# A hybrid convolution and attention block: attention output gated inside its units, one of two masks replaced by value differences, other starting points for attention and layer norm

## The chip, the cores and the metric

The kernel runs on one core of one Trainium2 chip. The metric is device time in microseconds (us) for one launch; three runs were taken before the change, and one further run was profiled. Engines are named as in the profile: PE is TensorE (PEld is its weight load), DVE is VectorE, ACT is ScalarE, POOL is GpSimd, and SP is SyncE, whose queue issues the DMAs.

## The reference

One decoder block over 2048 tokens of width 1024, in float32:

```python
h = rmsnorm(x, norm_g)
glu_in, conv_gate, q, k, v, attn_gate, merge_logits = split(h @ w_in)      # 7680 columns
c = silu(layernorm(causal_depthwise_conv31(a * sigmoid(b)) + b_dw))        # a, b = halves of glu_in
y_conv = (c * silu(conv_gate)) @ w_conv_out
a = attention(rope(q), rope(k), v)      # 16 heads of 64, 4 KV heads, window 128, a sink logit per head
y_attn = (a * silu(attn_gate)) @ w_attn_out
g_conv, g_attn = split(sigmoid(merge_logits))
x = x + (g_conv * y_conv + g_attn * y_attn) @ w_out
return rmsnorm(x, final_norm_g)
```

With a window of 128 and blocks of 128 queries, query q of a block sees key j of its own block where j <= q, and key j of the block before where j > q: 128 keys in all, one for each j.

## The kernel before

**Tiling.** The tokens are worked in two sweeps of 1024 (`sweep(s)`), and each sweep in two halves of 512. Activations lie transposed, channels on the partitions. Every float32 product is made of three float32r passes: a high and a low part are kept of both operands (`put_split`, `split_lo`; the low part is "full minus high"), and hi*hi, hi*lo and lo*hi are added in PSUM. A projection (`project`) takes 48 matmuls of 128x512: 8 channel blocks, 3 passes, 2 halves. Its result leaves PSUM through an `ev` function on ACT or DVE.

**Stages of a sweep.** First k, v and q with their rotary embedding (`rope_items`, `v_item`; item 12 of the list of items is the first gate), mixed with the GLU pairs (`gb` and `ga`, eight of them, at the places in `GLU_AFTER`). Then four kinds of gates (`ag`, `cg`, `ma`, `mc`, eight projections each), each written to DRAM by `gate_item` and read back by `load_gate`. Then `ya` (attention output times w_attn_out), `yc` (convolution branch times w_conv_out) and `o` (times w_out) with the final norm.

**What runs beside the projections.** `Line` keeps a clock in estimated us of PE work and decides where in PE's order other work is written. PE's order is exactly the written one; the order on the other engines and on SP is made by the framework's scheduler. In the background list `bg`, one operation is written every `line.every` us: the depthwise convolution (`conv_ops`, 31 DVE operations of 128x1024 for each of 8 channel blocks), later layer norm (`ln_center`, `ln_recip`, `ln_apply`) and the preparation of operands (`a_ops`, `u_ops`). Attention is 32 units a sweep (4 KV heads times 8 blocks), one every `ATT_EVERY`, each in three steps with `LAT` between them:

1. `sc`: 8 matmuls of scores; DVE lays the two blocks' scores into one 128x512 tile `ss` (by `copy_predicated`), takes the maximum; ACT takes exponentials and normalises.
2. `tpp`: 4 transposes; ACT and DVE split the result into `pt`; POOL makes `pc` (own block's part) from `pt` by one `affine_select`, and masks `pt` itself (block before) by a second one.
3. `ov`: 4 matmuls with `v_of(g, b)` and `v_of(g, b - 1)`, then ACT and DVE add the parts to `oT`, which is written to DRAM (`spill["att"]`).

**The operand of `ya`.** `a_op(e, h)` loads a half block of attention output (`latt`) and of its gate (`lag`) into two of the five `t2k` buffers, multiplies them on DVE, copies the high part on ACT and subtracts on DVE, into `aT[h][e]`. The 16 of them are written after the last unit, 14 through `bg` and 2 once layer norm has ended. `ya_item(0, True)` empties all lists (`line.finish()`) before its first matmul. The slots `AT[0]` to `AT[15]` hold the units' tiles and later `aT`.

Of the kernel before, what the change touches and what calls it, by code (L numbers as in the profile page):

```python
# [51 lines left out]
def hybrid_block(ctx: ExitStack, tc: tile.TileContext, x, par_d, w_in, w_conv, sinks, w_attn, w_out,  # L52
# [93 lines left out]
    def lnb(c):  # L146
# [10 lines left out]
    v_halo = const.tile([P, NKV, 2, HD], F32R, name="v_halo")


    class Line:  # L160
# [38 lines left out]
        def after(self, us, chain):  # L199
            self.late.append((self.t + us, chain, lambda: True))  # L200
# [162 lines left out]
    def sweep(s):  # L363
# [6 lines left out]
        glu_slot = [C[7], C[6], C[5], C[4], AT[14], AT[15], C[7], AT[14]]  # L370
# [71 lines left out]
        def rope_items(name, e, store):  # L442
# [7 lines left out]
            def ev_b(half, ps):  # L450
                a = first[half]
                b = slot(AT[6], [P, 2, TH], F32, f"rb{s}_{name}_{half}")
# [25 lines left out]
        vt = {}  # L478

        def v_item(i):  # L480
            def chain(half, vs):
                yield 0.0, 7.0
                tp = tp_ps.tile([P, 4, P], F32, tag="tp", name=f"tpv{s}_{i}_{half}")
                for j in range(4):
                    pe.transpose(out=tp[:, j, :], in_=vs[:, j * P:(j + 1) * P], identity=ident)
                for j in range(2):
# [3 lines left out]
                    src = tp[:, 2 * j:2 * j + 2, :].rearrange("p b (g d) -> p b g d", d=HD)  # L490
                    hi, lo = (vt[bp][:, :, 2 * i:2 * i + 2, a * HD:(a + 1) * HD] for a in range(2))
                    act.copy(hi, src)
                    split_lo(lo, src, hi, dve)
# [33 lines left out]

        def attention(n):
            g, b = divmod(n, NB)
            u = f"{s}_{g}_{b}"  # L530
# [14 lines left out]
            oT = ss[:, 512:768].rearrange("p (a q) -> p a q", q=P)  # L545
# [23 lines left out]
            for h in range(GQ):  # L569
                pe.transpose(out=tpp[:, h, :], in_=sb[:, h, :], identity=ident)  # L570
            pt = slot(next_of("pt", AT[7:9]), [P, 2, GQ, P], F32R, f"pt{u}")
# [4 lines left out]
            else:  # L576
# [3 lines left out]
                pool.affine_select(out=pt, in_=f(pt), pattern=[[0, 2], [0, GQ], [-1, P]],  # L580
                                   compare_op=ALU.is_gt, fill=0.0, base=0, channel_multiplier=1)
                seq = [(v_of(g, b), pc), (v_of(g, b - 1), pt)]
# [8 lines left out]
            for r, own, other in ((0, slice(0, HD), slice(HD, P)), (1, slice(HD, P), slice(0, HD))):  # L591
                act.copy(oT[own], ovp[other, :, r, :])
                dve.tensor_tensor(out=oT[own], in0=ovp[own, :, r, :], in1=oT[own], op=ALU.add)
# [58 lines left out]
        def ln_chain():  # L652
# [3 lines left out]
            ln["mu"] = slot(AT[15], [P, T], F32, f"mu{s}")  # L656
# [7 lines left out]
        def ln_chain2():  # L664
# [3 lines left out]
            ln["r"] = slot(AT[14], [P, T], F32, f"rstd{s}")  # L668
# [12 lines left out]
        line.every = CONV_EVERY  # L681
# [236 lines left out]
```

## Time and profile before

| | us |
|---|---|
| three runs | 2933.14, 2132.34, 2133.77 |
| median | 2133.77 |
| the profiled execution | 2133.61 |
| its span, first to last instruction | 2131.9 |

| engine | busy us | share of the span | instructions |
|---|---|---|---|
| PE | 2075.1 | 97% | 9256 |
| DVE | 1404.9 | 66% | 1804 |
| ACT | 1008.8 | 47% | 2195 |
| POOL | 576.8 | 27% | 396 |

The mean granted clock of PE was 0.978 of full speed. PE's matmuls are pipelined, so that its busy share also counts stretches in which it advances slowly; the number of matmuls in a stretch, the granted clock and the list of waits say more. What lies outside the span (1.7 us) belongs to the launch.

### The profile page before, as it was taken

How to read it: one execution, taken by the hardware profiler on the slowest of the kernel's cores; microseconds unless marked ns; L12 is line 12 of the kernel's file. 1: busy time of each engine (PE TensorE's matmuls, PEld its weight loads, DVE VectorE, ACT ScalarE, POOL GpSimd, SP SyncE). 2: the span in 40 equal slices, each digit the busy share in tenths (PEclk: the TensorE clock that was granted, in tenths of full speed). 3: DMA queues.
4: the chain of work that ended last, by engine and by line, in shares of the span. 5: the costliest groups of instructions: out<-in, count | busy, mean ns of one | idle time of the engine just before them, and what ended most of it. 6: DMA issues, size and time to landing. Idle time of an engine off the chain costs nothing.

```text
span 2131.9 us, 27345 instructions
## 1 busy us (share of the span) xinstructions
PE 2075.1 (97%) x9256; PEld 1680.3 (79%) x9256; DVE 1404.9 (66%) x1804; ACT 1008.8 (47%) x2195; POOL 576.8 (27%) x396
## 2 busy tenths in 40 slices
PE   7999999999999989999999999999999999899998
PEld 6877778888788865888888888888888888478887
DVE  4999997797693747123568899796696664351224
ACT  6211256666658863122442123767666779331222
POOL 2445534444443431242001121222222211000200
PEclk9999999999999996999999999999999999799999
DMA  7343554545446458545344356454555554774431
GB/s 249 129 138 120 159 168 136 173 134 158 150 136 185 149 177 266 163 143 212 109 149 139 119 172 189 149 161 138 157 153 150 167 149 144 241 249 135 142 125 79
DMA packets 231515, 339.11 MB, mean 159 GB/s; under 512 B 26576, under 2 KB 92240, under 8 KB 231376
## 3 DMA queue, kind: packets, MB, share of 16 engines
q1 hardware_dynamic: 231376, 337.37, 49.8%
q8 instruction: 73, 1.20, 0.2%
q14 instruction: 66, 0.54, 0.1%
HBM read 226.12 MB, written 111.15 MB: 158 GB/s over the span
## 4 chain that ended last, share of the span: by engine, by line
PE 76%; DVE 6%; DMA 3%; ACT 2%; issue 1%; POOL 0%; SPq 0%; DVEq 0%; ACTq 0%; POOLq 0%
PE o L839 8%; PE mm_yc L273 8%; PE mm_ma L273 8%; PE mm_ag L273 8%; PE mm_ya L273 8%; PE mm_ga L273 6%; PE mm_cg L273 6%; PE mm_gb L273 6%; PE mm_mc L273 5%; DVE cv L384 3%; DMA latt<-d_att 2%; PE sc L542 2%; PE ov L589 2%; PE mm_q_a L273 2%; PE mm_q_b L273 2%; PE tpp L570 1%
## 5 line engine op out<-in xcount | busy, mean ns | idle before, releaser
L384 DVE SCALAR_TENSOR_TENSOR cv<-glu,par,cv 128x1024 f32<-128x1024 f32 x480 | 694.9, 1448 | 7.6
L578 POOL TENSOR_SCALAR_AFFINE_SELECT pc<-pt 128x1024 fp32r<-128x1024 f32 x60 | 91.3, 1521 | 436.9 <-DVE pt L234 394.6
L273 PE MATMUL mm_ya<-aT,whi_ya 128*128 128x512 f32 x512 | 184.8, 437 | 21.8 <-ACT aT L287 19.6
L839 PE MATMUL o<-wo,mT 128*128 128x512 f32 x768 | 180.8, 394 | 0.0
L273 PE MATMUL mm_ga<-hT,whi_ga 128*128 128x512 f32 x512 | 163.4, 401 | 5.4 <-DVE rb_q__1_1318 L454 3.4
L839 PEld LDWEIGHTS o<-wo,mT 128*128 128x128 f32 x768 | 143.3, 188 | 31.5
L273 PE MATMUL mm_gb<-hT,whi_gb 128*128 128x512 f32 x512 | 161.8, 397 | 0.0
L273 PE MATMUL mm_ag<-hT,whi_ag 128*128 128x512 f32 x512 | 160.7, 395 | 0.0
L273 PE MATMUL mm_cg<-hT,whi_cg 128*128 128x512 f32 x512 | 160.7, 395 | 0.0
L273 PE MATMUL mm_ma<-hT,whi_ma 128*128 128x512 f32 x512 | 160.6, 395 | 0.0
L273 PE MATMUL mm_mc<-hT,whi_mc 128*128 128x512 f32 x512 | 160.2, 394 | 0.0
L273 PE MATMUL mm_yc<-uT,whi_yc 128*128 128x512 f32 x512 | 159.4, 392 | 0.0
L273 PEld LDWEIGHTS mm_ya<-aT,whi_ya 128*128 128x128 f32 x512 | 103.1, 201 | 71.2 <-ACT aT L287 38.3
L560 ACT ACTIVATE ss<-ss,st 128x128 f32<-128x128 f32 x256 | 99.9, 391 | 102.2 <-DVE st L555 101.4
L273 PEld LDWEIGHTS mm_ga<-hT,whi_ga 128*128 128x128 f32 x512 | 96.0, 191 | 27.2 <-issue 6.2
L273 PEld LDWEIGHTS mm_yc<-uT,whi_yc 128*128 128x128 f32 x512 | 96.2, 188 | 21.9
L273 PEld LDWEIGHTS mm_gb<-hT,whi_gb 128*128 128x128 f32 x512 | 95.8, 190 | 20.6
L273 PEld LDWEIGHTS mm_mc<-hT,whi_mc 128*128 128x128 f32 x512 | 95.1, 188 | 20.5
L776 POOL TENSOR_TENSOR lmc<-lmc,mp 128x512 f32<-128x512 f32 x32 | 42.0, 1311 | 253.8 <-DVE lmc L775 249.7
L273 PEld LDWEIGHTS mm_ag<-hT,whi_ag 128*128 128x128 f32 x512 | 94.4, 188 | 19.7
L273 PEld LDWEIGHTS mm_ma<-hT,whi_ma 128*128 128x128 f32 x512 | 94.4, 188 | 19.5
L273 PEld LDWEIGHTS mm_cg<-hT,whi_cg 128*128 128x128 f32 x512 | 94.1, 188 | 19.3
(357 smaller groups left out, 4420.1 us busy)
## 6 DMA issues: line engine op xcount, KB each, us to landing
qk<-d_q SPq DMA_DIRECT2D x256, 64.0 KB, 2.6
qk<-d_k SPq DMA_DIRECT2D x240, 64.0 KB, 2.4
raw_gb<-in_w_in_dram SPq DMA_DIRECT2D x34, 256.0 KB, 3.1
raw_ga<-in_w_in_dram SPq DMA_DIRECT2D x34, 256.0 KB, 3.9
raw_ag<-in_w_in_dram SPq DMA_DIRECT2D x32, 256.0 KB, 3.4
d_ag<-ag SPq DMA_DIRECT2D x32, 256.0 KB, 2.1
d_att<-ss SPq DMA_DIRECT2D x64, 128.0 KB, 2.1
raw_cg<-in_w_in_dram SPq DMA_DIRECT2D x32, 256.0 KB, 3.1
```

The lines of the kernel that those rows point to most:

```text
L273: pe.matmul(out=ps, lhsT=a, rhs=b, start=(k == 0 and i == 0), stop=(k == KC - 1 and i == 2))
L384: dve.scalar_tensor_tensor(out=cv[c], in0=glu[c][:, j:j + T], scalar=tap(c, j), in1=cv[c], op0=ALU.mult, op1=ALU.add)
L542: pe.matmul(out=o, lhsT=q[:, h, :], rhs=r, start=(j == 0), stop=(j == 1))
L560: act.activation(out=sb[:, h, :], in_=sb[:, h, :], func=AF.Exp, scale=SCALE, bias=ngm[:, h:h + 1], accum_out=den[:, h:h + 1])
L570: pe.transpose(out=tpp[:, h, :], in_=sb[:, h, :], identity=ident)
L578: pool.affine_select(out=pc, in_=f(pt), pattern=[[0, 2], [0, GQ], [1, P]], compare_op=ALU.is_ge, fill=0.0, base=0, channel_multiplier=-1)
L589: pe.matmul(out=ov, lhsT=vv, rhs=pp[:, i % 2], start=(i == 0), stop=(i == nm - 1))
L776: pool.tensor_tensor(out=g, in0=g, in1=mp[e][:, half * TH:(half + 1) * TH], op=ALU.add)
L839: pe.matmul(out=ps, lhsT=a[:, c0:c0 + P], rhs=r, start=(k == 0 and i == 0), stop=(k == KC - 1 and i == 2))
```

## The change

- **Gating in the unit.** Step 2 of a unit loads its piece of the attention gate (`ga`, 128x256) into a free part of `ss`. After `ov`, DVE multiplies `oT` by it, ACT copies the high part and DVE subtracts the low part, and both go to a new DRAM array `d_a`. `a_op` is now one DMA of 512 KB straight into `aT[h][e]`. Steps 2 and 3 of a unit are held until the gate's projection is stored.
- **Value differences.** With P the probabilities by j, the output is the sum over all j of P times v(block before), plus the sum over j <= q of P times (v(own block) - v(block before)). So `pt` stays unmasked, one `affine_select` (for `pc`) is left, and `v_item` makes the differences `vd` beside `vt`, in three new slots `X` and in `AT[15]`.
- **Order.** `GLU_AFTER`, the spacing constants and `LAT` change; the first unit falls into the first gate projection as before, but three GLU pairs stand ahead of it now, not four. `ROPE_EVERY` 3.2 holds until the units are planned, `CONV_EVERY` from there.
- **Layer norm** keeps its mean and scale in `X[0]` and `X[1]`; `ln_apply` is put at the end of the background list; the `u` operands are begun from a list of their own; `ya_item(0)` empties the lists only where an operand was not yet written.
- The GLU tiles take turns in three slots, the rotary part `rb` in two, and the GpSimd's DMA scratch is made smaller to make room.

```diff
-LN_LAT = (14.0, 30.0)
-LN_EVERY = 2.4
-GLU_AFTER = (0, 4, 8, 12, 16, 20, 24, 28)
+LN_LAT = (14.0, 24.0)
+LN_EVERY = 1.6
+GLU_AFTER = (0, 6, 12, 16, 19, 22, 25, 28)
+ROPE_EVERY = 3.2
 CONV_EVERY = 2.4
-ATT_EVERY = 14.5
-LAT = (22.0, 14.0)
+ATT_EVERY = 13.8
+LAT = (22.0, 16.0)
...
-        glu_slot = [C[7], C[6], C[5], C[4], AT[14], AT[15], C[7], AT[14]]
+        glu_slot = [C[7], C[6], AT[14], C[7], C[6], AT[14], C[7], AT[14]]
...
+                vf, d = (t2k(f"{n}{s}_{i}_{half}").rearrange("p (b c) -> p b c", c=P) for n in ("vf", "vd"))
+                act.copy(vf, tp)
+                dve.tensor_tensor(out=d[:, 1:4], in0=tp[:, 1:4], in1=vf[:, 0:3], op=ALU.subtract)
+                dve.tensor_tensor(out=d[:, 0], in0=tp[:, 0], in1=v_last[:, i], op=ALU.subtract)
+                act.copy(v_last[:, i], vf[:, 3])
...
+                    for full, to in ((tp, vt), (d, vd)):
+                        part = full[:, 2 * j:2 * j + 2, :].rearrange("p b (g d) -> p b g d", d=HD)
+                        hi, lo = (to[bp][:, :, 2 * i:2 * i + 2, a * HD:(a + 1) * HD] for a in range(2))
+                        act.copy(hi, part)
+                        split_lo(lo, part, hi, dve)
...
+            nc.sync.dma_start(out=ga, in_=spill["ag"][e2, :, qs].rearrange("c p q -> p c q"))
...
-                pool.affine_select(out=pt, in_=f(pt), pattern=[[0, 2], [0, GQ], [-1, P]],
-                                   compare_op=ALU.is_gt, fill=0.0, base=0, channel_multiplier=1)
-                seq = [(v_of(g, b), pc), (v_of(g, b - 1), pt)]
+                seq = [(v_of(g, b - 1), pt), (vd[b // 2][:, b % 2, g, :], pc)]
...
-            nc.sync.dma_start(
-                out=spill["att"][s * KC + 2 * g:s * KC + 2 * g + 2, :, b * P:(b + 1) * P].rearrange(
-                    "c p q -> p c q"),
-                in_=oT)
+            dve.tensor_tensor(out=oT, in0=oT, in1=ga, op=ALU.mult)
+            hl = sb.rearrange("p (l c) q -> p l c q", c=2)
+            act.copy(hl[:, 0].bitcast(F32R), oT)
+            split_lo(hl[:, 1].bitcast(F32R), oT, hl[:, 0], dve)
+            for i in range(2):
+                nc.sync.dma_start(out=d_a[e2, :, i, qs].rearrange("c p q -> p c q"), in_=hl[:, i])
...
-            line.bg.extendleft(reversed(work_ops))
+            line.bg.extend(work_ops + [lambda c=c: ln_apply(c) for c in range(KC)])
+            line.late.append((line.t, u_chain(), lambda: len(uT) > 0))
...
         def a_op(e, h):
             aT[h][e] = slot(AT[8 * h + e], [P, 2, TH], F32R, f"aT{s}_{h}_{e}")
-            gated(aT[h][e], "ag", e, h, lambda: load_gate("att", e, h))
+            nc.sync.dma_start(out=f(aT[h][e]), in_=d_a[s * KC + e, :, :, h * TH:(h + 1) * TH])
...
+        def a_chain():
+            for op in a_ops:
+                op()
+                yield 0.0, 1.5
+
+        def start_tail():
+            line.late.append((line.t, a_chain(), lambda: NKV * NB - 1 in done))
...
-        line.every = CONV_EVERY
+        line.every = ROPE_EVERY
...
             def first_blocks():
-                line.finish()
                 start_u()
+                if None in aT[0] + aT[1]:
+                    line.finish()
                 yield from blocks()
```

**Three places in the order.** The first is PE in the first sweep, where the last attention unit (`ov_3_7`) ends among the `mc` gates. Before:

```order
L273 MATMUL mm_mc_51_6652<-hT_1_7_318,wlo_mc_51_6509 128x512
L589 MATMUL ov_3_7_6686<-pc_3_7_6575,vt_3_794 128x512 x2
L589 MATMUL ov_3_7_6686<-pt_3_7_6572,vt_3_794 128x512 x2
L273 MATMUL mm_mc_60_6711<-hT_0_0_122,whi_mc_60_6610 128x512 x2
L273 MATMUL mm_mc_60_6711<-hT_0_0_122,wlo_mc_60_6611 128x512
```

The same place on PE after the change:

```order
L279 MATMUL mm_mc_20_6497<-hT_0_6_130,wlo_mc_21_6398 128x512
L611 MATMUL ov_3_7_6519<-pt_3_7_6384,vt_3_813 128x512 x2
L611 MATMUL ov_3_7_6519<-pc_3_7_6387,vd_3_814 128x512 x2
L279 MATMUL mm_mc_20_6497<-hT_0_7_131,whi_mc_21_6397 128x512 x2
L279 MATMUL mm_mc_20_6497<-hT_0_7_131,wlo_mc_21_6398 128x512
```

The last unit moves from behind `mc` projection 5 to the first half of projection 2. Up to the first matmul of `ya` stand 96 matmuls of 128x512 before the change and 275 after it; in the second sweep 105 and 284.

The second place is SP's queue near the end of attention in the first sweep. After the change the loads of `aT_<half>_<block>` stand among the stores of the last units (`d_a<-ss`), the gates' stores and the weights of `mc` projections 4 and 5:

```order
L248 DMA raw_mc_41_6611<-in_w_in_dram 128x512
L713 DMA aT_0_2_6571<-d_a 128x2x512
L713 DMA aT_0_7_6689<-d_a 128x2x512
L621 DMA d_a<-ss_3_6_6057 128x2x128 x2
L432 DMA d_mc<-mc_1_0_6442 128x512
L713 DMA aT_1_1_6744<-d_a 128x2x512
L713 DMA aT_0_6_6670<-d_a 128x2x512
L261 DMA d_lo<-wlo_mc_30_6488 128x512
L248 DMA raw_mc_50_6728<-in_w_in_dram 128x512
```

Before the change the pairs of loads begin behind the stores of `mc` projection 6:

```order
L424 DMA d_mc<-mc_6_1_6767 128x512
L430 DMA lag_0_0_6788<-d_ag 128x512
L430 DMA latt_0_0_6790<-d_att 128x512
L430 DMA lag_1_0_6808<-d_ag 128x512
L430 DMA latt_1_0_6810<-d_att 128x512
L255 DMA d_lo<-wlo_ya_00_6774 128x512
```

So the loads move ahead by several projections, and each of them waits only for its slot and for `d_a`.

The third place is DVE in the middle of attention, first sweep, after the change: the end of unit (1,1) and the beginning of unit (1,4) between operations of the convolution (`cv_4`).

```order
L615 TENSOR_TENSOR ss_1_1_3123<-ov_1_1_3500,ss_1_1_3123 64x256
L571 COPY_PREDICATED ss_1_4_3535<-causal,sc_1_4_3526 128x512
L616 TENSOR_TENSOR ss_1_1_3123<-ss_1_1_3123 128x256
L575 TENSOR_REDUCE st_1_4_3538<-ss_1_4_3535 128x4
L240 TENSOR_TENSOR ss_1_1_3123<-ss_1_1_3123 128x256
L576 SCALAR_TENSOR_TENSOR st_1_4_3538<-st_1_4_3538,nsink 128x4
L390 SCALAR_TENSOR_TENSOR cv_4_3495<-glu_4_3061,par,cv_4_3495 128x1024
```

The rows of L616 (times the gate) and L240 on `ss` (low part) are new; the second waits for ACT's copy of the high part, with one operation between them.

More of the change, by code (lines that the diff above doesn't have):

```diff
@@ L75, in hybrid_block @@
     C = [f"c{i}" for i in range(8)]
+    X = [f"x{i}" for i in range(3)]
     WIDE = set(C) | {"a14", "a15", "h14", "h15"}
@@ L197, in start, with after @@
             self.step(chain, ok)
-        def after(self, us, chain):
-            self.late.append((self.t + us, chain, lambda: True))
+        def after(self, us, chain, ok):
+            self.late.append((self.t + us, chain, ok))
         def finish_bg(self):
@@ L417, in glu_items @@
                     project(w_in[C_GLU_A // P + c], h_rhs, f"ga{s}_{c}", ev_a)]
+        stored = set()
         def gate_item(kind, col, func, e):
@@ L424, in ev @@
                 nc.sync.dma_start(out=spill[kind][s * KC + e, :, half * TH:(half + 1) * TH], in_=g)
+                if half == 1:
+                    stored.add((kind, e))
             return project(w_in[col // P + e], h_rhs, f"{kind}{s}_{e}", ev)
@@ L451, in ev_b @@
                 a = first[half]
[L452 removed]
+                b = slot(next_of("rb", [AT[6], AT[13]]), [P, 2, TH], F32, f"rb{s}_{name}_{half}")
                 dve.tensor_tensor(out=b[:, 1, :], in0=ps, in1=cs[half][:, 1, :], op=ALU.mult)
@@ L489, in chain @@
                         vt[bp] = slot(AT[bp], [P, 2, NKV, 2 * HD], F32R, f"vt{s}_{bp}")
[L490 to L493, printed above, removed]
+                        vd[bp] = slot((X + AT[15:])[bp], [P, 2, NKV, 2 * HD], F32R, f"vd{s}_{bp}")
+                    for full, to in ((tp, vt), (d, vd)):
[3 more added lines that the diff above has]
+                        split_lo(lo, part, hi, dve)
                 yield 0.44, 0.0
@@ L526, in load_qk @@
                                   in_=d_k[:, i % 2, fs, k0:k0 + nk].rearrange("a p t -> p a t"))
+        begun = set()
         def attention(n):
             g, b = divmod(n, NB)
+            begun.add(n)
             u = f"{s}_{g}_{b}"
@@ L544, in attention @@
             sb = ss[:, 0:512].rearrange("p (h q) -> p h q", q=P)
-            oT = ss[:, 512:768].rearrange("p (a q) -> p a q", q=P)
+            oT, ga = (ss[:, c:c + 256].rearrange("p (a q) -> p a q", q=P) for c in (512, 768))
             if first:
@@ L606, in start_attention @@
             for n in range(NKV * NB):
-                line.after(22.0 + n * ATT_EVERY, attention(n))
+                line.after(22.0 + n * ATT_EVERY, attention(n),
+                           lambda n=n: n not in begun or ("ag", 2 * (n // NB) + 1) in stored)
+            line.every = CONV_EVERY
+            start_tail()
         ln = {}
@@ L750, in ev @@
                 if half == 0:
+                    if ("u", e, 1) not in stored:
+                        line.finish()
                     mp[e] = slot(C[e], [P, T], F32, f"mp{s}_{e}")
```

58 lines of the change are left out of this document (30 added, 28 removed).

## The prediction

> **What bounds the kernel now.** I read the engines' busy times and the granted clock first, then the list of waits of PE, then a table of stretches.
>
> ```profile
> PE 2075.1 (97%) x9256; PEld 1680.3 (79%) x9256; DVE 1404.9 (66%) x1804; ACT 1008.8 (47%) x2195; POOL 576.8 (27%) x396
> ...
> PEclk9999999999999996999999999999999999799999
> ```
>
> PE is the bound. Its clock falls at two places, slices 16 and 35 of 40: the starts of `ya` in the two sweeps. The list of waits names what PE stood for:
>
> ```profile
> PE mm_ya L273 <- ACT aT L287: 19.6, 18, 3.2
> ...
> PE ov L589 <- POOL pc L578: 4.1, 2, 3.4
> PE mm_ga L273 <- DVE rb_q__1_1318 L454: 3.4, 1, 3.4
> PE mm_q_b L273 <- DVE ra_q__0_1693 L448: 2.6, 1, 2.6
> ...
> PE mm_ga L273 <- DVE rb_q__1_1811 L454: 1.9, 1, 1.9
> ...
> PE mm_q_b L273 <- DVE ra_q__0_1201 L448: 1.3, 1, 1.3
> ```
>
> The list understates `ya`, where PE also runs slowly. Stretches cut at its edges (length, then busy time and instructions of PE, PEld, DVE, ACT, POOL, clock, DMA share, GB/s) show it, beside a stretch of PE at full rate from the chain that ended last:
>
> ```profile
> 788.00:826.00 38.00, 27.64 (x49) 11.63 (x47) 22.24 (x31) 10.91 (x18) 3.30 (x3) 0.58 0.86 278
> 826.00:906.10 80.10, 80.10 (x340) 65.57 (x340) 34.54 (x49) 18.30 (x31) 18.47 (x14) 0.97 0.61 194
> ...
> 1831.50:1869.00 37.50, 26.04 (x49) 11.51 (x47) 18.73 (x29) 10.34 (x18) 0.00 (x0) 0.59 0.79 247
> 1869.00:1948.20 79.20, 79.20 (x340) 64.94 (x341) 30.51 (x47) 18.09 (x31) 0.00 (x0) 0.98 0.64 208
> ...
> 2036.74 88.45 PE o L839 x384
> ```
>
> At full rate a matmul costs 88.45 / 384 = 0.230 us. `ya` has 384 in each sweep, 88.4 us of work. From 788.0 to 906.1 it took 118.1 us, from 1831.5 to 1948.2 116.7: up to 29.7 and 28.3 us lost, 58 together; I count 57, since the first stretch opens with a few last matmuls of `mc`. Why it is slow, the chain shows, one operand `aT` after the other:
>
> ```profile
> 806.92 0.70 DVE lag L721
> 807.64 0.63 ACT aT L287
> 808.37 0.59 DVE aT L234
> 809.00 0.70 DVE lag L721
> 809.72 3.96 DMA latt<-d_att
> ```
>
> Load, product, copy, subtraction, and the next load waits for a buffer.
>
> **The change part by part.** All sums go against the profiled execution, 2133.6 us, which lies 0.2 below the median of 2133.77.
>
> *`aT` from DRAM ready-made.* The 32 products, copies and subtractions leave this place; 16 loads of 512 KB a sweep remain. The last unit ends 275 matmuls ahead of `ya` now (284 in the second sweep), not 96 (105): 275 x 0.230 = 63 us of cover. The 16 loads are 8.4 MB; at the 278 GB/s of the row above they take 30 us, and many start earlier, as slots come free. So nothing of them should be left at `ya`: gain 57, of which I keep back 3 for the order of the `u` operands, which now share DVE with `ya`'s own evacuations. **-54.**
>
> *Wider spacing in the rotary stage.* These two rows are the stretch in which PE waits for the rotary tiles `ra` and `rb`:
>
> ```profile
> 53.30:213.20 159.90, 154.58 (x671) 124.91 (x670) 153.11 (x127) 29.75 (x56) 77.32 (x48) 0.99 0.40 129
> 213.20:266.50 53.30, 48.82 (x202) 39.09 (x201) 51.52 (x41) 11.51 (x19) 28.40 (x18) 0.94 0.52 159
> ```
>
> DVE is busy 204.6 of 213.2 us: it is the late one. Now three GLU pairs, not four, stand ahead of attention, so that one convolution of some 44 us less is due here, at 3.2 us an operation instead of 2.4. The four waits (3.4 + 2.6 + 1.9 + 1.3 = 9.2) go, and with them the lowered clock, which costs its missing share of each stretch: 0.01 x 159.9 + 0.06 x 53.3 = 4.8. **-14.** The value differences add here, for 8 chains, two subtractions and two splits on DVE. The trace has no such subtraction; the nearest row is the split of the same size:
>
> ```profile
> L234 DVE TENSOR_TENSOR vt<-tpv,vt 128x256 fp32r<-128x256 f32 x16 | 6.7, 417 | 0.4 <-ACT vt L492 0.4
> ```
>
> With some 0.9 us for the two subtractions that is 1.7 us a chain, 7 a sweep, hidden in what the convolution leaves. Without that cover it would be 14.
>
> *One mask less.* PE waited 4.1 us for `pc`, and the clock was low there:
>
> ```profile
> 533.00:586.30 53.30, 49.90 (x222) 40.50 (x221) 35.20 (x51) 36.85 (x89) 21.45 (x17) 0.94 0.49 150
> ```
>
> That is 4.1 + 0.06 x 53.3 = 7.3. Only the last two of the four `ov` matmuls need `pc` now, and step 3 comes 2 us later by the planner: **-7.**
>
> *What VectorE has to do during attention.* This is the price. Per unit, DVE worked on `ss`, `st`, `pt` and `ov`:
>
> ```profile
> L550 DVE COPY_PREDICATED ss<-causal,sc 128x512 f32<-128x512 int32 x64 | 47.5, 742 | 44.3 <-ACT ss L549 41.5 <-DMA d_att<-ss 1.9
> L593 DVE TENSOR_TENSOR ss<-ov,ss 64x256 f32<-64x256 f32 x128 | 53.5, 418 | 71.3 <-ACT ss L592 70.0
> L234 DVE TENSOR_TENSOR pt<-tpp,pt 128x512 fp32r<-128x512 f32 x64 | 43.7, 683 | 59.4 <-ACT pt L572 59.2
> ...
> 260.00:800.00 540.00, 54.07 (x160) 0.99 0.50 157
> ```
>
> The last row is the five operations on `st` alone, of 32 units: 1.69 each. So 0.74 + 2 x 0.42 + 0.68 + 1.69 = 3.95 us. The product with the gate and the new split are 128x256, by the `vt` row 0.42 each: 4.8 us. From one GLU pair to the next there are five projections now (six before) and some 4.8 units. PE needs 5 x 48 x 0.2303 = 55.3, and per unit these three rows, 2.30 us:
>
> ```profile
> 449.52 0.44 PE tpp L570 x4
> 450.66 0.92 PE ov L589 x4
> 455.78 0.94 PE sc L542 x8
> ```
>
> Together 66.3 us. In that time DVE has one convolution, 31 operations:
>
> ```profile
> L384 DVE SCALAR_TENSOR_TENSOR cv<-glu,par,cv 128x1024 f32<-128x1024 f32 x480 | 694.9, 1448 | 7.6
> ...
> L384 DVE SCALAR_TENSOR_TENSOR cv<-glu,par,cv x480: 1255/1285/2391, 54.0 to 1676.5; 128x1024 f32<-128x1024 f32 x160
> ...
> 440.32 1.28 DVE L384 SCALAR_TENSOR_TENSOR cv<-glu,par,cv 128x1024 f32<-128x1024 f32 x1
> 441.52 0.17 DVE L563 RECIPROCAL st<-st 128x4 f32<-128x4 f32 x1
> ```
>
> By the mean, 31 x 1.45 + 4.8 x 4.8 + 1.4 (two GLU evacuations of some 0.7) = 69.4 us, 105% of PE's time. But the last two rows overlap: the operation of 1.28 us is followed after 1.20. With 0.08 off each long operation and the small ones unchanged, 31 x 1.37 + 4.8 x 4.4 + 1.2 = 64.8, 98%. So DVE is just full. Four such periods a sweep: by the first figure it falls behind 3.1 x 4 = 12 us a sweep, of which the 22 us that the planner leaves between steps 1 and 2 take up most; by the second nothing. The lower figure is the nearer, as starts in a full stretch show it. I take **+5** for both sweeps, bounds 0 and 25.
>
> The convolution also gets lighter. Its median is 1.285, its mean 1.448: 480 x 0.163 = 78 us of excess. The Trainium skill, GPSIMD Engine Reference, Specifications, says that GpSimd's SBUF interfaces are shared with VectorE, with contention for DVE instructions that have two SBUF inputs, as these have. If the excess is spread over POOL's busy time, the removed mask has this part in it:
>
> ```profile
> L580 POOL TENSOR_SCALAR_AFFINE_SELECT pt<-pt 128x1024 fp32r<-128x1024 f32 x60 | 88.6, 1477 | 3.8
> ```
>
> 78 x 88.6 / 576.8 = 12 us, 0.75 a convolution, an estimate from rows; it moves the 69.4 to 68.6 and leaves the term within its bounds.
>
> *The rest* I cost at nothing: layer norm gets a shorter plan (by its constants 8 x 1.6 + 24 = 37 us from mean to scale, not 8 x 2.4 + 30 = 49) in a stretch that attention has left; SP has more to issue, and a load of `aT` can hold up weights behind it, but those stand two projections, 22 us, ahead. Uncovered, the two would cost some 5 us each.
>
> Sum: 2133.6 - 54 - 14 - 7 + 5 = **2063.6**; I forecast 2063. Within 2% of 2133.77 (2091.1 to 2176.4) is about what a measurement of this kernel cannot tell from no change.
>
> **The rivals.**
>
> *VectorE becomes the bound in attention.* For: it was the late engine in the rotary stage, where it was busy 96%; if it gets no further than 96% here, 69.4 / 0.96 = 72.3 us a period, 6 over PE's 66.3, or 24 a sweep. In the first sweep alone, where POOL also makes the low parts of the weights: 2063.6 - 5 + 24 = 2083. In both: 2107, within 2%. Against: the overlap above, and that much of the mean comes from the rotary stage. 0.08 for the first and 0.08 for the second.
>
> *The operands still come late.* If the loads waited for the end of attention's queue and ran in front of `ya`, 30 us a sweep would stay of the 57 in all, so that -54 nearly vanishes: 2117. Against: the 275 matmuls. Beside it, the clock: in the slow stretches it was 0.58, though the longest single wait of PE there was 3.2 us. If the low clock belonged to the place and not to the waits, it would cost 0.42 x 38.0 + 0.41 x 37.5 = 31 us: 2095. Against: from 906 to 1818 PE is fed and no slice shows less than 9 tenths. The Trainium skill, TensorE: Matmul & The Clock Gate, section "What's actually happening", gives idle windows of some 3.4 us as the cause of the half clock, so that a fed PE keeps the full one: by it this second case does not occur, and the trace agrees outside `ya`. 0.05 for both.
>
> *Slower than before: DVE stands in the unit.* The new split waits for ACT's copy, in order, with everything behind it: the next unit's reductions, the convolution. The row of L593 shows such a wait now, 70.0 us before 64 units, 1.1 each. DVE has (66.3 - 64.8) / 4.8 = 0.3 us to spare a unit. To eat the whole gain of 70 + 5, over some 62 units, each must stand 1.2 + 0.3 = 1.5 us longer; to end 2% slower (2176.4), (2176.4 - 2058.6) / 62 + 0.3 = 2.2 us, twice the like wait now. A stand of 2.4 us gives 2058.6 + 62 x 2.1 = 2189. 0.04.
>
> **How the numbers follow.** Forecast, 2050 to 2078: 0.72. VectorE late in one sweep, 0.08, still faster; in both, 0.08, within 2%. Operands or clock, 0.05, within 2%. DVE standing, 0.04, slower. Below 2050, all terms at their best: 0.03. The unknown costs (+5 up to +25, layer norm and SP 5 each) take the upper end to 2063 + 30 = 2093, and I set it at 2092; the lower end is 2050. Faster by over 2%: 0.72 + 0.08 + 0.03 = 0.83; within 2%: 0.13; slower: 0.04.
>
> **What would show it.** At the start of `ya` the stretch should have the clock at 0.97 or more and some 231 matmuls in 53.3 us, no wait for `aT`, and no loads `latt` or `lag`. The waits for `ra` and `rb` should be gone and DVE below 85% in the rotary stage. In attention DVE should be busy over 90% throughout the first sweep; long waits there of `tpp`, `ov` or `mm_ga` for DVE would be the first rival. The mean of the convolution's operations should fall below 1.448. The forecast is wrong above all if attention's stretch loses more than 30 us.

## The result and the profile after

The changed kernel took 2097.57 us (median of four runs, 2097.0 to 2100.21), the kernel before 2133.12 in runs on the same chip: a ratio of 0.9837, 95% interval 0.9818 to 0.9856. It is 1.6% faster, where 2063 was forecast, 3.3%, and lies above 2092, the upper end that the prediction gave. Single runs of 2933 us above and 4226 us in experiment 7 stand far from all others and do not move the medians. The profiled execution took 2100.2 us, against 2133.6 before: 33.4 us won, of the 70 that the sum had.

The busy times and the granted clock on the page of the changed kernel:

```profile
PE 2049.7 (98%) x9256; PEld 1673.3 (80%) x9256; DVE 1394.8 (66%) x1901; ACT 1012.8 (48%) x2251; POOL 477.9 (23%) x336
...
PEclk9999999999999999999999999999999999999999
```

The two slices with a low clock are gone. `ya` now begins at 807.3 and 1826.6 us and ends at 899.7 and 1914.2; each sweep's `ya` in two stretches (length, then busy time and instructions of PE, PEld, DVE, ACT, POOL, clock, DMA share, GB/s):

```profile
807.30:845.30 38.00, 34.83 (x151) 27.70 (x150) 24.43 (x32) 19.61 (x29) 8.94 (x6) 1.00 0.60 192
845.30:899.70 54.40, 54.20 (x237) 44.10 (x236) 10.56 (x16) 8.65 (x14) 14.13 (x11) 1.00 0.60 204
1826.60:1864.10 37.50, 37.50 (x166) 30.84 (x165) 24.17 (x38) 15.73 (x27) 0.00 (x0) 1.00 0.85 272
1864.10:1914.20 50.10, 50.10 (x221) 41.20 (x220) 6.22 (x9) 5.59 (x9) 0.00 (x0) 1.00 0.50 167
```

It takes 92.4 and 87.6 us, where 88.4 is the work and 118.1 and 116.7 was the time. That part of the forecast came out. What came out otherwise is in the first sweep. The list of waits, first PE's (without its first row, the start of the kernel), then ACT's:

```profile
PE mm_ma L279 <- ACT glu L412: 3.9, 1, 3.9
PE mm_q_b L279 <- DVE rb_q__1_1524 L464: 3.4, 1, 3.4
PE mm_ya L279 <- DVE mp L788: 3.4, 3, 1.8
PE mm_ga L279 <- ACT ag L431: 2.9, 1, 2.9
PE mm_cg L279 <- ACT glu L412: 2.6, 1, 2.6
...
PE ov L611 <- POOL pc L602: 0.4, 1, 0.4
...
ACT ss L614 <- DVE ss L615: 97.5, 57, 5.8
ACT ss L618 <- DVE ss L616: 97.2, 58, 3.8
```

No `aT` is in it, and `pc` is down from 4.1 to 0.4 us. New are waits for ACT to empty a PSUM tile (`glu`, `ag`). ACT, in its turn, stands for DVE at the two places in a unit's end where the two hand over to each other; before the change its longest stand for DVE, 101.4 us in all, was the one for the maximum of the scores.

To see the losses that no wait shows (a lowered clock, small gaps), I add up, for each stage, the distance from each matmul's start to the next, less what a matmul of its shape takes at full rate (0.2303 us for 128x512). These are the microseconds that PE loses by stage; the figures 0 and 1 are the sweeps, "rotary" is the stage of k, v and q, "attention" reaches from the first scores to the first matmul of layer norm. A small negative figure is the error of the method.

| kernel | rotary 0 | attention 0 | LN 0 | ya 0 | rotary 1 | attention 1 | LN 1 | ya 1 | all |
|---|---|---|---|---|---|---|---|---|---|
| before | 16.4 | 11.0 | 1.7 | 29.1 | 0.9 | 2.6 | 0.5 | 27.7 | 100.1 |
| after | 10.3 | 34.4 | 4.4 | 3.9 | 0.9 | 3.8 | 0.1 | -0.8 | 66.7 |

"All" takes in the start and the last stages (some 10 us in each kernel). The difference of 33.4 us is just that of the two profiled times. So nearly the whole result lies in four numbers: `ya` won 25.2 and 28.5 us, the rotary stage 6.1, and the first sweep's attention lost 23.4. The second sweep's attention, with the same units, lost 1.2. In either kernel it has no wait of PE and a clock of 1.00, so that 2 to 4 us in attention belong to the method.

Two stretches of 450 us, in the two sweeps' attention, in the changed kernel, and the first in the kernel before:

```profile
250.00:700.00 450.00, 431.77 (x1999) 351.50 (x1998) 389.77 (x509) 295.91 (x709) 157.08 (x106) 0.98 0.52 160
1150.00:1600.00 450.00, 450.00 (x2088) 371.29 (x2087) 368.26 (x498) 253.46 (x586) 76.36 (x48) 1.00 0.56 168
```

```profile
250.00:700.00 450.00, 445.41 (x2086) 367.46 (x2086) 347.85 (x437) 293.31 (x686) 204.42 (x134) 0.99 0.50 156
```

DVE is busy 390 of 450 us in the first sweep, 348 before, 368 in the second sweep. How that reaches PE shows the order of time, around a wait of 2.9 us of PE. First DVE, then ACT, then POOL, then PE (start, duration):

```profile
352.14 3.67 DVE L390 SCALAR_TENSOR_TENSOR cv<-glu,par,cv 128x1024 f32<-128x1024 f32 x2
355.73 0.69 DVE L240 TENSOR_TENSOR pt<-tpp,pt 128x512 fp32r<-128x512 f32 x1
356.33 3.31 DVE L390 SCALAR_TENSOR_TENSOR cv<-glu,par,cv 128x1024 f32<-128x1024 f32 x2
359.56 0.41 DVE L615 TENSOR_TENSOR ss<-ov,ss 64x256 f32<-64x256 f32 x1
...
361.70 0.96 DVE L616 TENSOR_TENSOR ss<-ss 128x256 f32<-128x256 f32 x1
```

```profile
354.56 0.37 ACT L614 COPY ss<-ov 64x256 f32<-64x256 f32 x1
360.00 0.36 ACT L614 COPY ss<-ov 64x256 f32<-64x256 f32 x1 [5.07 <-DVE ss L615]
...
362.70 0.41 ACT L618 CAST ss<-ss 128x256 fp32r<-128x256 f32 x1 [1.69 <-DVE ss L616]
...
366.18 1.28 ACT L431 ACT_TABLE_LOAD   x1
367.48 0.60 ACT L431 ACTIVATE ag<-mm_ag 128x512 f32<-128x512 f32 x1
```

```profile
352.12 1.30 POOL L240 TENSOR_TENSOR wlo_gb<-raw_gb,whi_gb 128x512 fp32r<-128x512 f32 x1 [2.68 <-ACT whi_gb L251]
356.49 2.07 POOL L602 TENSOR_SCALAR_AFFINE_SELECT pc<-pt 128x1024 fp32r<-128x1024 f32 x1 [3.08 <-DVE pt L240]
```

```profile
368.12 0.85 PE L279 MATMUL mm_ga<-hT,whi_ga 128*128 128x512 f32 x2 [2.90 <-ACT ag L431]
```

DVE has no gap. Two taps (operations of the convolution, L390) take 3.67 us and the next two 3.31 there, instead of 2 x 1.28, and it is just then that POOL works. The unit's sum comes 5 us after ACT asked for it, ACT stands 5.07 and 1.69 us, the gate's tile is emptied late, and PE has no free PSUM tile to write to. Before it empties the tile ACT also loads a function table twice, 1.28 us each; but it makes 63 such loads in this stretch of 450 us in experiment 2 too, against 62 here, and there PE loses next to nothing.

### The profile page after: what moved, and what is told of

Read it like the earlier page. It is cut to its first block, busy times and chain, and to the rows that moved or that the text cites. A ratio compares the mean times of both kernels' runs of the same rounds, so it can differ in the third digit from the quotient of the medians.

```text
span 2098.5 us, 27434 instructions
## 1 busy us (share of the span) xinstructions
PE 2049.7 (98%) x9256; PEld 1673.3 (80%) x9256; DVE 1394.8 (66%) x1901; ACT 1012.8 (48%) x2251; POOL 477.9 (23%) x336
## 4 chain that ended last, share of the span: by engine, by line
PE 79%; DVE 11%; DMA 3%; ACT 3%; issue 2%; POOL 1%; SPq 1%; DVEq 0%; ACTq 0%; POOLq 0%
PE mm_ma L279 9%; PE o L874 8%; PE mm_yc L279 8%; PE mm_ya L279 7%; PE mm_ag L279 7%; PE mm_gb L279 7%; PE mm_mc L279 7%; DVE cv L390 6%; PE mm_ga L279 6%; PE mm_cg L279 6%; PE mm_q_b L279 3%; PE mm_q_a L279 3%; PE sc L563 2%; PE ov L611 2%; PE mm_v L279 1%
## 5 line engine op out<-in xcount | busy, mean ns | idle before, releaser
L390 DVE SCALAR_TENSOR_TENSOR cv<-glu,par,cv 128x1024 f32<-128x1024 f32 x480 | 682.5, 1422 | 6.3
L602 POOL TENSOR_SCALAR_AFFINE_SELECT pc<-pt 128x1024 fp32r<-128x1024 f32 x60 | 102.4, 1707 | 430.0 <-DVE pt L240 428.2
L874 PEld LDWEIGHTS o<-wo,mT 128*128 128x128 f32 x768 | 143.0, 188 | 32.1
L279 PE MATMUL mm_ya<-aT,whi_ya 128*128 128x512 f32 x512 | 159.1, 392 | 3.4 <-DVE mp L788 3.4
L279 PEld LDWEIGHTS mm_ya<-aT,whi_ya 128*128 128x128 f32 x512 | 95.8, 188 | 25.6 <-DVE mp L788 3.1
L614 ACT COPY ss<-ov 64x256 f32<-64x256 f32 x128 | 47.0, 367 | 119.9 <-DVE ss L615 97.5
```

The source lines that it names most:

```text
L279: pe.matmul(out=ps, lhsT=a, rhs=b, start=(k == 0 and i == 0), stop=(k == KC - 1 and i == 2))
L390: dve.scalar_tensor_tensor(out=cv[c], in0=glu[c][:, j:j + T], scalar=tap(c, j), in1=cv[c], op0=ALU.mult, op1=ALU.add)
L602: pool.affine_select(out=pc, in_=f(pt), pattern=[[0, 2], [0, GQ], [1, P]], compare_op=ALU.is_ge, fill=0.0, base=0, channel_multiplier=-1)
L874: pe.matmul(out=ps, lhsT=a[:, c0:c0 + P], rhs=r, start=(k == 0 and i == 0), stop=(k == KC - 1 and i == 2))
```

## The experiments

All ratios are to the kernel before, run on the same chip in the same turn; "lost" is a number of the table's kind. Unless said otherwise an edit is made to the changed kernel.

**1. The unit's high part on DVE.** If ACT's standing for the product is the cause, this removes one of its two turns.

```diff
-            act.copy(hl[:, 0].bitcast(F32R), oT)
+            dve.tensor_copy(out=hl[:, 0].bitcast(F32R), in_=oT)
```

> The changed kernel with one edit: the copy of the gated output's high part is made by VectorE, not ScalarE. In the changed kernel ScalarE stands 97 us in all for VectorE's product before this copy, and PE then waits in the first sweep's attention for ScalarE's evacuations of gates and GLU parts. Theory A (ScalarE stands in its queue for the product, and the PSUM evacuations behind it are late): this standing goes, PE's waits of some 28 us in that stretch fall by 10 us or more, 2080 to 2088. Theory B (VectorE is full there, and whatever waits for it is late): VectorE gets 64 more operations of some 0.3 us, no gain, 2096 to 2108.

Measured 2093.02 us, 0.9815 (0.9798 to 0.9831). Attention 0 lost 29.5 instead of 34.4: neither theory's figure. ACT's turn for the product is at most a small part, 4.9 us.

**2. No low parts made by POOL.** In the first sweep POOL makes the low part of each weight and stores it; the second sweep loads it. Here 148 of the 152 are loaded in the first sweep too (the first weight's low parts stand for all).

```diff
+            elif (0, kh) in lo_stored:
+                nc.sync.dma_start(out=f(lo), in_=d_lo[0, kh])
             else:
                 split_lo(lo, raw, hi, pool)
```

> The changed kernel, but in the first sweep the low parts of the weights (all but the first two) are loaded from DRAM, from the first weight's low part, so that GpSimd makes none of them. The low parts are so not those of the weights; the work on PE, ScalarE and VectorE stays the same in number. The first sweep then has GpSimd's load of the second, in which PE lost nothing. Theory C (GpSimd's work slows VectorE's operations, and that makes the first sweep's VectorE too full): the convolution's operations fall from 1.42 us to about 1.33 in the mean, the waits of the first sweep's attention (some 28 us) and of its rotary stage (some 8) nearly vanish: 2062 to 2072. If GpSimd's part in it is small and the density of the convolution alone decides: 2088 to 2098.

Measured 2053.9 us, 0.9629 (0.9615 to 0.9644): some 44 us less, more than expected. Rotary 0 lost 0.3 and attention 0 lost 3.6. PE's stretch is full, with DVE at 349 us instead of 390:

```profile
250.00:700.00 450.00, 450.00 (x2134) 372.84 (x2133) 348.83 (x520) 310.70 (x740) 65.08 (x45) 1.00 0.69 219
```

**3. The GLU pairs at their old places.** `GLU_AFTER` back to (0, 4, 8, 12, 16, 20, 24, 28), all else as changed.

> The changed kernel with the places of the GLU pairs as before, (0, 4, 8, 12, 16, 20, 24, 28): four pairs ahead of attention and six projections from pair to pair. Theory B (density of the convolution against attention on VectorE): the first sweep's waits in attention fall from some 28 us to 10 to 15, those of the rotary stage rise from 8 to 12 to 15: 2085 to 2092. Theory D (the new steps in a unit make it late whatever the density): no less waiting in attention and more in the rotary stage, 2098 to 2106.

Measured 2121.06 us, 0.9944 (0.9929 to 0.9959). Both theories failed: rotary 0 lost 20.2, where the kernel before loses 16.4, attention 0 still 27.8, LN 1 4.1, and `ya` 0 15.7, most of it in one wait of PE:

```profile
PE mm_ya L279 <- DVE mp L788: 13.6, 1, 13.6
```

So pairs three items apart instead of four account for 6.6 of the 34.4 us, and the new places are worth 23 us by themselves: 9.9 are won in the rotary stage, 11.8 in `ya` and 4.0 in LN 1, against those 6.6.

**4. Two masks again.** The value differences are taken out, the second `affine_select` put back.

```diff
...
-                seq = [(v_of(g, b - 1), pt), (vd[b // 2][:, b % 2, g, :], pc)]
+                pool.affine_select(out=pt, in_=f(pt), pattern=[[0, 2], [0, GQ], [-1, P]],
+                                   compare_op=ALU.is_gt, fill=0.0, base=0, channel_multiplier=1)
+                seq = [(v_of(g, b), pc), (v_of(g, b - 1), pt)]
```

> The changed kernel with the value differences undone: two masks on GpSimd for a unit, the own block's values as before, no differences in the value stage; all else as changed. If the mask's time on GpSimd and its contention with VectorE matter, as the prediction's 7 us and its 12 us of relief say: 2104 to 2118, the convolution's mean back at 1.44. If they don't: 2094 to 2100, the differences' own work in the value stage (PE waits 2.2 us there) gone.

Measured 2105.27 us, 0.9868 (0.9853 to 0.9883): the value differences bring some 7 us, though the two intervals just touch. Attention 0 lost 42.4 instead of 34.4; PE now waits for `pt` from POOL, and the taps' mean is 1.436 us:

```profile
PE ov L607 <- POOL pt L598: 8.1, 8, 2.3
```

**5. The gate back in the tail.** The unit stores the bare output, and product and split come before `ya`, as background work.

```diff
-            dve.tensor_tensor(out=oT, in0=oT, in1=ga, op=ALU.mult)
...
-                nc.sync.dma_start(out=d_a[e2, :, i, qs].rearrange("c p q -> p c q"), in_=hl[:, i])
+            nc.sync.dma_start(out=spill["att"][e2, :, qs].rearrange("c p q -> p c q"), in_=oT)
...
-            nc.sync.dma_start(out=f(aT[h][e]), in_=d_a[s * KC + e, :, :, h * TH:(h + 1) * TH])
+            gated(aT[h][e], "ag", e, h, lambda: load_gate("att", e, h))
```

> Everything as in the changed kernel (value differences, the new places of gate pairs and units, LN in its own slots), but the unit stores the bare output again, and the gate product and the split come back as background work before the attention projection. The first sweep's attention lost 34.4 us of TensorE time in the changed kernel and 11.0 before; ya lost 29.1 and 27.7 before, 3.9 and -0.8 in the changed kernel. Theory G (the 0.84 us that the gate and the split add to VectorE in each unit, with their round trip over ScalarE, are what the first sweep's attention pays): attention of sweep 0 loses 8 to 18, ya about 27 in each sweep, 2118 to 2130 us. Theory P (the attention's loss comes from units put 13.8 instead of 14.5 us apart and the later gate pairs, whatever a unit does): attention still loses over 27, ya about 27 each, 2138 to 2152 us.

Measured 2148.68 us, 1.0066 (1.005 to 1.0081). Attention 0 lost 14.1 instead of 34.4, as theory G said: the gate in the unit costs 20 us there. `ya` lost 28.6 and 24.6, and layer norm 12.5 and 6.7, which I had not counted, so that the time lies not in theory G's range but in theory P's, whose attention did not come. So gating in the unit brings some 50 us, after having paid those 20.

**6. The kernel before, without POOL's low parts.** The edit of experiment 2.

> The kernel before, with one difference: the low parts of the first sweep's weights are loaded (those of the first weight stand for all, so its output is not the reference's), and GpSimd makes four of them instead of 168. In the changed kernel the same edit took 43.7 us. Theory C (GpSimd's low parts slow VectorE, and what that costs depends on how full VectorE is): in before only the waits of its first sweep's rotary stage (16.4) and attention (11.0) can go, and the ya stages keep their 29 and 28: 2104 to 2116 us. Rival (the low parts cost about the same 40 us in either kernel, for instance through the queue or the transfers): 2085 to 2098 us. Rival 2 (the cost is a matter of the new units alone): 2125 to 2134 us.

Measured 2109.99 us, 0.9886 (0.987 to 0.9903): 24.2 us, theory C. Rotary 0 lost 0.3 instead of 16.4 and attention 0 2.7 instead of 11.0; `ya` kept 30.9 and 27.0. The same work of POOL, 148 low parts (the 168 of the expectation should be 152), costs 24 us in the kernel before and 44 in the changed one.

**7. Half the convolution in the first sweep.** The taps 1 to 30 run on 512 of 1024 positions.

```diff
-                dve.scalar_tensor_tensor(out=cv[c], in0=glu[c][:, j:j + T], scalar=tap(c, j),
-                                         in1=cv[c], op0=ALU.mult, op1=ALU.add)
+                n = T if s else TH
+                dve.scalar_tensor_tensor(out=cv[c][:, 0:n], in0=glu[c][:, j:j + n], scalar=tap(c, j),
+                                         in1=cv[c][:, 0:n], op0=ALU.mult, op1=ALU.add)
```

> The changed kernel with the convolution's taps 1 to 30 of the first sweep done on the first 512 of the 1024 positions only (the other half keeps tap 0's value, so the output is not the reference's): same number of instructions in the same order and places, each about half as long, GpSimd's low parts all kept. VectorE has some 150 us less to do between the first projections and the layer norm. Theory F (what GpSimd's work costs, it costs by filling VectorE, so that room on VectorE alone makes up for it): the rotary stage and the attention of the first sweep lose under 8 us together instead of 44.7, 2050 to 2066 us. Theory Q (it is GpSimd's own queue, or the ScalarE round trips in a unit, that TensorE ends up waiting for, full VectorE or not): they still lose 25 or more, 2078 to 2097 us.

Measured 2062.49 us, 0.9661 (0.9645 to 0.9677). Rotary 0 lost 6.4 and attention 0 3.7, 10.1 together: a little over theory F's 8, far below theory Q's 25. POOL still made all low parts:

```profile
250.00:700.00 450.00, 450.00 (x2136) 372.69 (x2135) 290.46 (x521) 312.37 (x748) 145.92 (x114) 1.00 0.57 180
```

Room on DVE alone makes up for POOL's work. So neither POOL's own queue nor the hand-overs of ACT and DVE cost by themselves.

**8. High part on DVE, units 14.5 us apart.** Experiment 1 with `ATT_EVERY` back at 14.5.

> The changed kernel with the unit's high part made on VectorE (2093.0 us by itself) and the units 14.5 us apart as before instead of 13.8. Theory D (units closer together fill VectorE beyond what it can do in the first sweep): attention of sweep 0 falls from 29.5 to about 18, the last unit ends some 20 us later in the order but still ahead of ya, 2080 to 2087 us. Rival (the work a unit brings is the same at either spacing and VectorE is behind anyway, or what is won in attention goes to a wait for the last units' outputs in ya): 2090 to 2100 us.

Measured 2113.02 us, 0.99 (0.9885 to 0.9914): a miss for both theories. Attention 0 lost 30.3, hardly another figure than 29.5, and layer norm 15.8 and 5.8. The distance of the units does not decide it; what was added appears in layer norm.

**9 to 11. Taking ACT out of DVE's way.** In 9 the two ACT copies of a unit come ahead of the two DVE sums; 10 adds the high part on DVE; 11 adds the first tap on ACT.

```diff
                 act.copy(oT[own], ovp[other, :, r, :])
-                dve.tensor_tensor(out=oT[own], in0=ovp[own, :, r, :], in1=oT[own], op=ALU.add)
+            for r, own in ((0, slice(0, HD)), (1, slice(HD, P))):
+                dve.tensor_tensor(out=oT[own], in0=ovp[own, :, r, :], in1=oT[own], op=ALU.add)
```

```diff
-                dve.tensor_scalar(out=cv[c], in0=glu[c][:, 0:T], scalar1=tap(c, 0), scalar2=cbias(c),
-                                  op0=ALU.mult, op1=ALU.add)
+                act.activation(out=cv[c], in_=glu[c][:, 0:T], func=AF.Identity, scale=tap(c, 0),
+                               bias=cbias(c))
```

> The changed kernel with the two ScalarE copies of a unit's output ahead of the two VectorE sums, instead of copy, sum, copy, sum; the same instructions otherwise. In the changed kernel ScalarE stood 97.5 us in 57 turns for the first sum before its second copy. Theory S (VectorE is late by a few microseconds at times, and that reaches TensorE because ScalarE stands for it at the head of its queue with evacuations behind): attention of sweep 0 loses about half or less of its 34.4 us, 2070 to 2084 us. Theory F (VectorE is short of time in the first sweep as a whole, and TensorE stands by what VectorE lacks whichever queue shows it): attention still loses 28 or more, 2090 to 2100 us.

> The same with the high part of the unit's gated output made on VectorE as well, so that ScalarE has nothing to wait for VectorE in a unit's end. Theory S: attention of sweep 0 loses under 10 us, 2062 to 2075 us. Theory F: VectorE has one instruction more in each unit, attention loses 25 or more as with the high part on VectorE alone (29.5), 2086 to 2096 us.

> The same again with the convolution's first tap (1024 columns with scale and bias, 0.98 us in the changed kernel) moved from VectorE to ScalarE: 8 us of VectorE's time per sweep. Theory F: VectorE's time is what counts, some 8 to 15 us less than the kernel with the copies first and the high part on VectorE. Theory S: within 4 us of that kernel.

Measured 2090.04 (0.9795, 0.978 to 0.9809), 2094.35 (0.9815, 0.9798 to 0.9831) and 2091.37 us (0.9802, 0.9787 to 0.9816); attention 0 lost 27.7, 32.1 and 28.4. ACT's wait for the sum is gone in 9, and its wait for the product has grown; in 10 both are gone, and ACT stands for DVE further on, for the maximum of the scores. ACT's list in 9, then in 10, and the stretch in 10:

```profile
ACT ss L619 <- DVE ss L617: 130.6, 58, 6.1
```

```profile
ACT ss L581 <- DVE st L576: 161.4, 48, 7.2
```

```profile
250.00:700.00 450.00, 428.88 (x2008) 348.95 (x2008) 399.64 (x538) 287.29 (x686) 164.47 (x108) 1.00 0.52 162
```

For 9 and 10 that is theory F: most of what is taken from one hand-over appears at the next. In 11 theory F failed: the first tap on ACT is worth 3.0 us, not the 8 to 15 expected, and within theory S's 4. The kernel of 9 beats the changed one (its interval ends below the other's start) and is, with 11 close by, the fastest version here that leaves no work out.

**12 and 13. Work moved, none taken away.** Pairs after items 16, 20, 24, 28 and 32, taps 2.65 us apart; in 12 with the copies first, in 13 on the changed kernel.

```diff
-GLU_AFTER = (0, 6, 12, 16, 19, 22, 25, 28)
+GLU_AFTER = (0, 6, 12, 16, 20, 24, 28, 32)
-CONV_EVERY = 2.4
+CONV_EVERY = 2.65
```

> The kernel with the copies first (2090.0 us, 27.7 lost in the first sweep's attention), with the last five gate pairs of a sweep four items apart (after items 16, 20, 24, 28 and 32 instead of 16, 19, 22, 25 and 28) and the taps' spacing raised from 2.4 to 2.65 us: the last convolution then stands beside units 26 to 29 instead of 22 to 25 in VectorE's order. No work goes. Theory R (the loss is one of place): attention of sweep 0 loses 6 to 14, ya nothing new, 2068 to 2077 us. Rival T (VectorE lacks the time in the first sweep whatever the order): attention and the layer norm together still lose 24 or more, 2086 to 2096 us. Rival L (the convolutions then end too late for the layer norm, and yc waits): attention falls, but 10 us or more appear behind it, 2080 to 2095 us.

> The same places on the changed kernel itself (copies and sums alternating as it has them). Theory R: attention of sweep 0 loses 12 to 20 instead of 34.4, 2076 to 2086 us. Rivals T and L: 2093 us or more.

Measured 2129.07 (0.9977, 0.9967 to 0.9987) and 2138.4 us (1.0019, 1.001 to 1.0028). Attention 0 lost 18.3 instead of 27.7, and 26.5 instead of 34.4; but `ya` lost 31.6 and 19.2 in 12, and 31.2 and 19.4 in 13. The time of 12 lies above the ranges of theory R and of both rivals. In kind it is rival L, though in `ya` and not in `yc`, and far dearer: `ya` writes its result into the slots of `cv`, and so waits until the `u` operands, with layer norm ahead of them, are through. PE's row and the stretch in 12:

```profile
PE mm_ya L279 <- DVE mp L789: 29.5, 4, 8.8
```

```profile
800.00:850.00 50.00, 32.80 (x112) 25.09 (x113) 44.23 (x53) 26.50 (x35) 5.84 (x4) 0.77 0.57 188
```

DVE's work in the first sweep can be eased by moving it only as far as `ya` allows, and these places went too far. Whether a smaller shift wins was not tried.

## Why the prediction was right or wrong

*`aT` ready-made, -54: right.* 29.1 + 27.7 became 3.9 - 0.8, which is -53.7.

*Rotary stage, -14: mis-sized, -6.1.* Of the four waits, 9.2 us, 5.2 are left (3.4 for `rb`, 1.3 and 0.5 for `ra`), and DVE is not below 85%. The same stretches as in the prediction, now:

```profile
53.30:213.20 159.90, 152.50 (x662) 123.31 (x661) 145.50 (x139) 35.15 (x72) 74.28 (x47) 0.99 0.44 142
213.20:266.50 53.30, 53.30 (x247) 43.95 (x246) 38.09 (x41) 23.48 (x52) 20.82 (x17) 1.00 0.63 195
```

The second is healed, the first is not: DVE is busy 145.5 of 159.9 us, 91% (86% over both rows, 96% before). I had taken one convolution out of the stage and let the taps come 3.2 us apart; on DVE they stand closer. There are 27 taps between 60 and 120 us and 25 between 140 and 200, 2.2 to 2.4 us apart, with DVE busy 59 of the 60 us each time and idle for 12 us in between. And I had not put POOL's price into this stage: without its low parts the stage loses 0.3.

*One mask less, -7: right in size.* Experiment 4 gives some 7, the wait for `pc` fell from 4.1 to 0.4. The size is partly luck: what the second mask costs in experiment 4 is 8.1 us of waits for `pt`, not the wait for `pc` and the clock from which I had made the 7.

*VectorE in attention, +5 for both sweeps: this step failed.* With the -7 it should have made attention lose 2 us less; it lost 23.4 more in the first sweep and 1.2 in the second. The balance of DVE against PE for a period of 66.3 us had wrong durations in it, and the lower figure was the wrong choice. DVE's groups in the first sweep's attention (busy, mean of one), then in the second's:

```profile
L390 DVE SCALAR_TENSOR_TENSOR cv<-glu,par,cv 128x1024 f32<-128x1024 f32 x172 | 251.8, 1464 | 1.9
L616 DVE TENSOR_TENSOR ss<-ss 128x256 f32<-128x256 f32 x28 | 25.3, 902 | 0.1
...
L240 DVE TENSOR_TENSOR pt<-tpp,pt 128x512 fp32r<-128x512 f32 x30 | 20.6, 686 | 30.2 <-ACT pt L596 30.2
...
L240 DVE TENSOR_TENSOR ss<-ss 128x256 fp32r<-128x256 f32 x28 | 15.5, 555 | 0.2 <-ACT ss L618 0.2
```

```profile
L390 DVE SCALAR_TENSOR_TENSOR cv<-glu,par,cv 128x1024 f32<-128x1024 f32 x178 | 239.1, 1343 | 2.2
...
L616 DVE TENSOR_TENSOR ss<-ss 128x256 f32<-128x256 f32 x20 | 10.0, 500 | 0.0
L240 DVE TENSOR_TENSOR ss<-ss 128x256 fp32r<-128x256 f32 x20 | 8.5, 425 | 0.3 <-ACT ss L618 0.3
```

I priced product and split at 0.42 each, by the split of `vt`. That operation has one input in PSUM; the product and the new split have both in SBUF. In the first sweep they take 0.90 + 0.56 = 1.46 us a unit, in the second 0.50 + 0.43 = 0.93. A period of the first sweep is then 31 x 1.464 + 4.8 x (3.95 + 1.46) + 1.4 = 72.8 us for DVE against PE's 66.3: 6.5 too much, in four periods 26 us; less the 7 of the mask that is 19, where 23.4 were lost. In the second sweep it is 31 x 1.343 + 4.8 x (3.95 + 0.93) + 1.4 = 66.5, which is PE's time, and 1.2 were lost. So full durations fit in size, without the overlap that I took off.

The sum is not shown to be the mechanism, though. DVE idled 60 of the 450 us above, which an engine short of time throughout would not do. For experiment 3, with six projections and some 5.8 units between pairs, the same sum gives 31 x 1.464 + 5.8 x 5.41 + 1.4 = 78.2 us for DVE and 79.7 for PE, so that nothing should be lost, and 27.8 were. Two stretches of its trace (columns as above):

```profile
300.00:350.00 50.00, 50.00 (x238) 41.40 (x238) 34.03 (x51) 33.56 (x77) 19.34 (x14) 1.00 0.47 151
350.00:400.00 50.00, 46.54 (x221) 37.50 (x219) 48.77 (x61) 31.24 (x80) 15.38 (x11) 1.00 0.47 149
```

DVE idled 16 of the first 50 us, so it owed nothing from the rotary stage any more; in the next 50 it was full, with 26 taps 1.9 us apart where the plan has 2.4, and PE fell behind. So DVE is late while the taps of a convolution run and has idle time between, which a balance over the whole period cannot show. Whether DVE's order, with the taps as far apart as planned, would take the loss away was not tried by itself.

*The rivals.* The first rival, DVE late in the first sweep alone, where POOL makes the low parts, is what happened. It was priced at 24 us, and had 0.08; the 24 came from 69.4 us and a DVE that stops at 96%, where the rows give 72.8 and 87%, so that the figure is near by luck. Its 2082.6 has -7 + 24 = +17 for attention; 6.4 more there, 7.9 that did not come in the rotary stage, 2.7 in the first layer norm and 0.6 in all the rest make the 2100.2 of the profiled execution. Experiments 2, 5 and 7 say that it takes both, POOL's work and a full DVE: with the low parts, the gate or half the convolution out, attention loses 3.6, 14.1 or 3.7. The rival of late operands did not occur, nor did the low clock stay with the place (1.00 in all four rows of `ya`), nor did DVE's standing in the unit: DVE idled 0.2 us before its 28 new splits. It was ACT that stood.

*What should show it.* `ya`'s clock and the missing loads: as said. Its first 53.3 us hold 215 matmuls in the first sweep, short of the 231 because PE waits 3.4 us for `mp`, and 235 in the second. The sign that I named above all others came, attention losing more than 30 us: 34.4. DVE "over 90% throughout the first sweep": it was 87% (389.8 of 450), and PE was late all the same: in pieces of 25 us DVE was busy for up to 24.8, in others for 16 to 21. The mean of the taps fell from 1.448 to 1.422:

```profile
L390 DVE SCALAR_TENSOR_TENSOR cv<-glu,par,cv 128x1024 f32<-128x1024 f32 x480 | 682.5, 1422 | 6.3
```

That is 480 x 0.026 = 12.5 us, the 12 that I had put down to the mask; but with two masks, in experiment 4, the mean was 1.436, so that about half of it is the mask's.

The Trainium skill, GPSIMD Engine Reference, Specifications, states that GpSimd's SBUF interfaces are shared with VectorE, with contention for DVE instructions with two SBUF inputs. The prediction put this rule on the removed mask alone, and not on the new operations. The trace agrees with it: the split of `pt`, with one input in PSUM, takes 0.686 us with POOL's low parts and 0.686 without; the product, with two in SBUF, takes 0.902 and 0.579, the taps 1.464 and 1.328. The rows of experiment 2:

```profile
L392 DVE SCALAR_TENSOR_TENSOR cv<-glu,par,cv 128x1024 f32<-128x1024 f32 x164 | 217.8, 1328 | 1.8
...
L240 DVE TENSOR_TENSOR pt<-tpp,pt 128x512 fp32r<-128x512 f32 x32 | 22.0, 686 | 42.6 <-ACT pt L598 42.5
...
L618 DVE TENSOR_TENSOR ss<-ss 128x256 f32<-128x256 f32 x31 | 18.0, 579 | 0.2
```

## What to carry to other kernels

Price a new operation by a row with the same places of its inputs, PSUM or SBUF, and with the same neighbours at work on the other engines; a row of the same size is not enough. When a sum for two engines comes out at 98 to 105%, it is not "just full" at no cost: take the full durations, stage by stage and sweep by sweep, and look at the stretches in which the work of one engine is bunched. And where a list of waits names an engine that hands on (here ACT for DVE), changing the hand-over moves the wait; only less work on the late engine, or less in its way, takes it off.

## What the runs showed of the hardware

POOL's operations slow the DVE's taps beside them from 1.28 to some 1.7 or 1.8 us (pairs of 3.67 and 3.31, beside a low part and beside the mask). The 148 low parts that experiments 2 and 6 leave out, some 1.5 us each, were worth 44 us of the whole time in the changed kernel (DVE busy 390 of 450 us) and 24 in the kernel before (348).

A short wait of PE can halve its clock for a while after it. After 1.80 us without work the granted clock was 0.50 and then full again (stretches of the changed kernel, columns as above):

```profile
782.40:784.40 2.00, 0.24 (x2) 0.00 (x0) 0.00 (x0) 0.60 (x1) 1.45 (x2) 1.00 0.47 159
784.40:786.00 1.60, 1.56 (x5) 1.27 (x6) 0.00 (x0) 1.58 (x2) 0.00 (x0) 0.69 0.85 292
786.00:788.40 2.40, 2.40 (x7) 1.85 (x6) 1.98 (x2) 2.25 (x3) 0.00 (x0) 0.50 0.76 226
788.40:792.00 3.60, 3.60 (x17) 2.91 (x16) 3.60 (x3) 0.60 (x1) 0.00 (x0) 1.00 0.00 0
```

At 0.69 and 0.50 that is 0.31 x 1.6 + 0.50 x 2.4 = 1.7 us on top of the 1.8. The wait is shorter than the idle windows of which the prediction speaks. Not every such wait does it: right behind one of 2.2 us for `vs`, from 93 to 97 us, the clock was 1.00. In the first sweep's attention the list names 18.2 us of waits, where 34.4 were lost. The clock was 0.93 in three pieces of 25 us and 0.86 in one, which makes (3 x 0.07 + 0.14) x 25 = 8.8 us more, and 3.8 is what the method shows in the second sweep without any wait; the last 3.6 are not accounted for.
